# Half-rows of conditioning moved from an RWKV layer into the MLP before it

## The chip, the core and the metric

The kernel runs on one core of one Trainium2 chip. The metric is the device time of one execution in microseconds; the median of several executions is compared. The engines are named as in the profile: PE is the matrix engine (PEld are its weight loads), DVE the vector engine, ACT the scalar engine, POOL the GpSimd engine, SP the engine whose queue issues nearly all DMA transfers here.

## What is computed

Two layers of an encoder on 256 tokens of width 2048, in float32. Each layer has a mixing part and an MLP of width 8192, and each of these four parts is conditioned: a vector c gives a shift, a scale and a gate per channel.

```
def adaln(x, c, norm_g, ada_w, ada_b):
    m = jax.nn.silu(c) @ ada_w + ada_b
    shift, scale, gate = jnp.split(m[:, None, :], 3, axis=-1)
    return rmsnorm(x, norm_g) * (1.0 + scale) + shift, gate

def sqrelu_mlp(h, w1, w2):
    return jnp.square(jax.nn.relu(h @ w1)) @ w2
...
        h, gate = adaln(x, c, tm_norm_g[i], tm_ada_w[i], tm_ada_b[i])
        y = rwkv7_block(h, ...)
        x = x + gate * y
        h, gate = adaln(x, c, ffn_norm_g[layer], ffn_ada_w[layer], ffn_ada_b[layer])
        x = x + gate * sqrelu_mlp(h, ffn_w1[layer], ffn_w2[layer])
```

The order of the parts is: mixing of layer 0 (a long convolution and a linear attention; "mix"), first MLP ("f0"), mixing of layer 1 (RWKV-7; "tm"), second MLP ("f1"), final norm. The conditioning matrix of each part is 2048 x 6144, so its product with silu(c) reads 50 MB for one vector; it depends on c alone and can be done at any time before the part needs it.

## The kernel before

**The conditioning in half-rows.** The matrix of each part is stored transposed and cut into tiles of 128 x 1024, 512 KB each, called half-rows here. A third of a part (0 shift, 1 scale, 2 gate) has 32 of them. `ada_load` issues the transfer of the next one on SP's queue into the pool `wp` (6 buffers); `ada_half` multiplies it on DVE with silu(c), which lies broadcast in SBUF, and sums along the row (line 362, one SCALAR_TENSOR_TENSOR). After each four columns of 128 the sums get their bias in a few small operations (lines 367 to 370). `bg` does one half-row: it keeps up to AP = 5 transfers ahead and then multiplies the oldest.

**When half-rows are done.** Each weight load (`load`, line 494) adds half the rate of the part to a counter in `tick`, and each whole unit calls `bg`. The rate of the first MLP is RF0 = 1.2, that of the second RF1 = 0.8. The first MLP's counter starts at DV = -12. In the RWKV layer the rate is 0, and the loop over pairs of heads calls `bg` instead: from pair 3 to pair 14, up to 10 or 5 times a pair (`bg_gen`, table BG). Which half-row comes next is set in `ada_load`: first the gate of the part that is running, once its shift and scale are done; then, over all parts in order, shift and scale. The gate of a later part is therefore never loaded before that part runs.

**The MLP.** `ffn` works in two halves. Each half has 8 blocks of w1 (`feat_block`, 8 weight tiles of 128 x 1024 each) and 4 blocks of w2 (`tok_block`, 16 tiles each): 256 weight tiles in an MLP. Every tile is split into a high part (a cast on ACT, line 465) and the rest (a subtraction on DVE, line 466), into three pairs of buffers, and each product is three matmuls (lines 510 to 512). Weight tiles go to 7 buffers of their own and, each seventh, to `wp`. The names are f_w (a tile, a weight's or a half-row's), f_wh and f_wl (its parts), f_h (normed input), f_hid (hidden).

**The RWKV layer.** After the norm, projections and a stretch of preparation comes a loop over 16 pairs of heads. In it `weave` mixes five streams: the chain of one pair (states Q, masks M, S), the preparation of the next, the tail of the one before, the linear blocks (`rw_v`, `rw_o`, three tiles loaded ahead into `wp`) and the half-rows. tm_M is a masked score of a pair, written by DVE (line 1506) and read by PE (line 1561). The gate is spread over the tokens after the last pair (`spread_gate`) and used in the residual.

**The order.** The program is written as above; a scheduler then sets the order of each engine's instructions. In a run each engine, and SP's queue, goes through its list in order: an instruction that waits holds up all behind it.

Of the kernel before, what the change touches and what calls it, by code (L numbers as in the profile page):

```python
# [25 lines left out]
SUBS = ("mix", "f0", "tm", "f1")  # L26
FX, FN, NU, XD = 2, 3, 0, 4
PT = ("0111111", "0111")
RHY, RGL, RWO, RF0, RF1 = 2.4, 2, 0.6, 1.2, 0.8
HA, HB, HN, HT = 1000, 1000, 0, 0  # L30
LG, MK, XS, TB, DU, RP, IB, L1, MP, AP = 2, 7, 4, 0, -8.0, 1, 3, 0, 3, 5
W1, W2 = 1, 1
BG, IV, CH, MT, B0, B1, M0, M1, LD = (10, 10, 10, 10, 10, 10, 10, 10, 10, 5, 5, 5, 5, 5, 5, 5, 5, 5), 12, 7, (5, 5, 5, 5, 5, 5, 5, 5, 5, 5, 5, 2, 3, 2, 3, 2, 3, 2), 3, 14, 6, 6, 6
PK, PF = 8, 3
RH, ZZ = (0, 2.4, 2, 2), 0
NF, F1, TF = 2, 2, 0
PR, PQ = 'mppp', 'mppp'
# [176 lines left out]
class Build:  # L214
# [21 lines left out]
    def run(self):  # L236
        nc, ctx, A = self.nc, self.ctx, self.A
        self.const = self.pool(ctx, "const")
        self.wp = self.pool(ctx, "wp", bufs=6)
        self.due, self.rate, self.turn, self.hold, self.starting = 0.0, 0.0, 0, None, False  # L240
        self.cut, self.casts, self.wq = None, [], None
        self.small = self.pool(ctx, "small", bufs=2)
        self.tmp = self.pool(ctx, "tmp", bufs=4)
        self.gstack = ctx.enter_context(ExitStack())
        self.open_gate()
        self.wstack = ctx.enter_context(ExitStack())
        self.open_work()
        self.mm = self.pool(ctx, "mm", bufs=4, space=PSUM)
        self.q = {"sp": nc.sync, "act": nc.scalar, "pool": nc.gpsimd}[QM]
        self.pstack = ctx.enter_context(ExitStack())  # L250
        self.open_ps(4)
        self.xstack = ctx.enter_context(ExitStack())
        self.ada_left = {(s, i): 2 * KT for s in self.stages if s in SUBS for i in range(3)}
        self.ada_next, self.ada_sum, self.ada_out, self.ada_done = [], {}, {}, {}
        self.label = self.stages[0]
        if self.stages[0] != "mix":
            self.start()
            self.load_x()
        for s in SUBS:
            if s in self.stages:  # L260
                self.label = s
                self.rate = RF0 if s == "f0" else RF1
                if s[0] == "f":
                    self.ffn(s)
                elif s == "mix":
                    self.mix()
                else:
                    self.rwkv()
        self.final()
# [43 lines left out]
    def ada_load(self):  # L313

        left, s = self.ada_left, self.label
        todo = [(s, 2)] if not left.get((s, 0)) and not left.get((s, 1)) else []
        if s == "mix" and left.get((s, 0)):
            todo = [(s, 0 if left[s, 0] % 2 or left[s, 0] == left[s, 1] else 1)]
        if self.starting:
            todo = [("mix", i) for i in range(2)] if not todo or todo[0][1] == 2 else todo  # L320
        else:
            todo += [(q, i) for q in SUBS for i in range(2)]
        for u in todo:
            if left.get(u):
                w = self.t(self.wp, [P, D // 2], "w")
                i, j = divmod(2 * KT - left[u], 2)
                self.nc.sync.dma_start(w, self.A["ada_" + u[0]][u[1] * KT + i][:, j])
                left[u] -= 1
                return *u, i, w, j
# [83 lines left out]
    def norm_t(self, s, split=True):  # L413
        h, step = self.norm_steps(s, split)
        for k2 in range(KT // 2):
            step(k2)
        return (lambda k: [a[:, k % 8, :] for a in h[k // 8]]) if split else h
# [44 lines left out]


    def split(self, a, hi, lo, eng=None):
        c = self.nc.scalar.copy(hi, a)  # L465
        d = (eng or self.nc.vector).tensor_tensor(lo, a, hi, ALU.subtract)  # L466
        if eng is None:
            self.cut = d.ins
            self.casts = [c.ins]

    def behind(self):

# [15 lines left out]
    def load(self, name, n, i, pools):  # L488

        self.turn += 1  # L490
        w = self.t(pools[self.turn % len(pools)], [P, 2, NB], "w")
        src = self.A[name][n, i // 2][:, i % 2 * 2 : i % 2 * 2 + 2]
        if self.wq is None:
            self.dma = self.nc.sync.dma_start(w, src).ins
        else:
            with self.tc.issue_after(self.casts[-1]):
                self.wq.dma_start(w, src)
        self.tick(self.rate / 2)
        return w

# [551 lines left out]
    def rwkv_out(self, yd, ns, k0, k1, pts, pool):  # L1052
# [18 lines left out]
        def ahead(u):  # L1071
            i, n = units[u]
            if i not in x:
                x.clear()
                x[i] = [self.t(self.xt, [P, 2, T], t, dt=F32R) for t in ("xh", "xl")]
                y = self.t(self.xt, [P, 2, T], "xu", bufs=2)
                nc.sync.dma_start(y, yd[:, 2 * i : 2 * i + 2, :])
                self.split(y, *x[i], nc.gpsimd)
            if u + 1 < len(units):
                load(u + 1)  # L1080
            v = [self.t(self.ws, [P, 2, NB], t, dt=F32R) for t in ("wh", "wl")]
            self.split_weights(w[u], v)
            return x[i], v

        def ready(u):
            return u == len(units) or self.tails >= min(2 * units[u][0] + 2, 14)

        load(0)
        while not ready(0):
            yield 1  # L1090
# [13 lines left out]
    def rwkv(self):  # L1104
# [12 lines left out]
        with ExitStack() as st:  # L1117
# [37 lines left out]
            with ExitStack() as st2:  # L1155
                self.hp = self.pool(st2, "hp", bufs=4, reuse_waits="tile")
                h, norm = self.norm_steps("tm", False)
                xx = [self.t(self.hp, [P, 8, T], "h") for _ in range(2)]
                for k2 in range(8):
                    norm(k2)  # L1160
                    a, o = (z[k2 // 4][:, 2 * k2 % 8 : 2 * k2 % 8 + 2] for z in (h, xx))
                    (nc.vector if k2 < XD else nc.gpsimd).tensor_tensor(o[:, :, 1 : T - 1], a[:, :, : T - 2], a[:, :, 2:], ALU.add)
                    nc.gpsimd.tensor_copy(o[:, :, 0], a[:, :, 1])
                    nc.gpsimd.tensor_copy(o[:, :, T - 1], a[:, :, T - 2])
                    nc.vector.scalar_tensor_tensor(o, o, 0.5, a, ALU.mult, ALU.subtract)
                nc.scalar.dma_start(xs, self.x)
                self.xstack.close()
                self.rate, self.wq = 0.0, None
                mixes = self.spill_mixes(h, xx)
                for _ in range(8):  # L1170
                    next(mixes)
                self.weave((self.lora(h, xx), 16), (mixes, 16), (self.take(mains, 35), 35))
# [23 lines left out]
            with ExitStack() as st1:  # L1196
# [69 lines left out]
                w = None  # L1266
                for n in range(4):
# [3 lines left out]
                    w = self.load("rw_o", n, KT // 2 - 1, [self.wp])  # L1271
# [3 lines left out]
                        for m in range(2):  # L1275
                            self.prod(pts[n][m], [a[:, k, m * P : (m + 1) * P] for a in y], [a[:, k, :] for a in v], False, k == 1)
                    self.residual("tm", n, pts[n])
        self.wq = None
        self.open_gate()
        self.open_work()  # L1280

# [444 lines left out]
```

## Time and profile before

| | before |
|---|---|
| median of 3 runs | 3051.21 us (3048.9 to 3052.1) |
| profiled execution | 3047.34 us, span 3045.3 us |
| PE busy, weight loads | 2871.4 us (94%), 2488.7 us (82%) |
| DVE busy | 2122.1 us (70%) |
| ACT busy | 1301.6 us (43%) |
| POOL busy | 522.2 us (17%) |
| moved by DMA | 752.30 MB, mean 247 GB/s |

The span is from the first instruction to the last; the profiled execution's own time is 2.0 us more. Busy shares are averages over stages of different kind. Line numbers are those of the kernel before.

### The profile page before, as it was taken

Reading aid. Unit: us, or ns where it says so; the run is one execution under the profiler, and the core shown is the slowest. Engines: PE = TensorE matmul, PEld = TensorE weight load, DVE = VectorE, ACT = ScalarE, POOL = GpSimd, SP = SyncE. Lnnn points to the kernel's source line nnn. Section 1 sums busy time; section 2 is a strip of 40 time slices with the busy share of each in tenths; the row PEclk is TensorE's granted clock in tenths of the full one; section 3 lists DMA queues with packets and bytes.
Section 4 is the critical chain, followed back from the end, with each engine's and each line's share of the span. In section 5 each row is a group of like instructions: output and inputs, shape, how many; then the busy total and the mean of one; then the engine's idle time right before and its main releaser. Section 6 shows DMA issues by size and latency. Waiting matters only on the chain. (4 is left out here: it accounts for less than half of the span.)

```text
span 3045.3 us, 52042 instructions
## 1 busy us (share of the span) xinstructions
PE 2871.4 (94%) x20308; PEld 2488.7 (82%) x20308; DVE 2122.1 (70%) x3126; ACT 1301.6 (43%) x1947; POOL 522.2 (17%) x574
## 2 busy tenths in 40 slices
PE   6999989999999999997999878999998999999998
PEld 2678776789988999886888777777778998899986
DVE  7899866657777788787768875775646776455454
ACT  3233334444443444443466542334445443344443
POOL 1211200011100011004354541322322110001000
PEclk9999999999999999998999987999999999999999
DMA  9978777747898988984987788997545777555552
GB/s 328 326 271 284 243 262 263 247 154 244 287 308 306 304 290 290 313 297 158 323 264 249 266 258 226 301 300 208 149 149 194 245 252 272 193 186 183 202 193 93
DMA packets 279970, 752.30 MB, mean 247 GB/s; under 512 B 73081, under 2 KB 99577, under 8 KB 278572
## 3 DMA queue, kind: packets, MB, share of 16 engines
q1 hardware_dynamic: 279148, 745.38, 73.1%
q8 instruction: 159, 2.61, 0.3%
q10 hardware_dynamic: 576, 3.60, 0.3%
q14 instruction: 87, 0.71, 0.1%
HBM read 706.08 MB, written 42.80 MB: 246 GB/s over the span
## 5 line engine op out<-in xcount | busy, mean ns | idle before, releaser
L466 DVE TENSOR_TENSOR f_wl<-f_w,f_wh 128x1024 fp32r<-128x1024 f32 x512 | 630.8, 1233 | 444.3 <-ACT f_wh L465 433.4
L465 ACT CAST f_wh<-f_w 128x1024 fp32r<-128x1024 f32 x512 | 538.0, 1052 | 748.4 <-PE f_mm L512 315.8
L511 PE MATMUL f_mm<-f_h,f_wh 128*128 128x256 f32 x2048 | 579.5, 283 | 0.0
L510 PE MATMUL f_mm<-f_h,f_wh 128*128 128x256 f32 x2048 | 579.5, 283 | 0.0
L512 PE MATMUL f_mm<-f_h,f_wl 128*128 128x256 f32 x2048 | 579.1, 283 | 0.0
L511 PE MATMUL f_mm<-f_wl,f_hid 128*128 128x512 f32 x1024 | 398.6, 389 | 1.1 <-DVE f_wl L466 1.1
L512 PE MATMUL f_mm<-f_wh,f_hid 128*128 128x512 f32 x1024 | 398.5, 389 | 0.0
L511 PEld LDWEIGHTS f_mm<-f_h,f_wh 128*128 128x128 f32 x2048 | 393.2, 192 | 0.1
L510 PEld LDWEIGHTS f_mm<-f_h,f_wh 128*128 128x128 f32 x2048 | 393.0, 192 | 0.1
L512 PEld LDWEIGHTS f_mm<-f_h,f_wl 128*128 128x128 f32 x2048 | 392.9, 192 | 0.0
L510 PE MATMUL f_mm<-f_wh,f_hid 128*128 128x512 f32 x1024 | 357.9, 389 | 0.0
L362 DVE SCALAR_TENSOR_TENSOR mix_w<-mix_w,mix_s 128x1024 f32<-128x1024 f32 x175 | 219.8, 1265 | 77.0 <-DMA mix_w<-in_ada_f 52.5
L466 POOL TENSOR_TENSOR f_hid<-f_u,f_hid 128x512 fp32r<-128x512 f32 x64 | 98.0, 1531 | 990.6 <-ACT f_hid L465 988.2
L362 DVE SCALAR_TENSOR_TENSOR f_w<-f_w,mix_s 128x1024 f32<-128x1024 f32 x174 | 233.6, 1345 | 2.6 <-DMA f_w<-in_ada_f 2.6
L511 PEld LDWEIGHTS f_mm<-f_wl,f_hid 128*128 128x128 f32 x1024 | 192.2, 188 | 41.3 <-DVE f_wl L466 1.7
L512 PEld LDWEIGHTS f_mm<-f_wh,f_hid 128*128 128x128 f32 x1024 | 192.3, 188 | 39.8
L510 PEld LDWEIGHTS f_mm<-f_wh,f_hid 128*128 128x128 f32 x1024 | 192.2, 188 | 39.7
L466 DVE TENSOR_TENSOR tm_wl<-tm_w,tm_wh 128x1024 fp32r<-128x1024 f32 x128 | 164.4, 1287 | 85.8 <-ACT tm_wh L465 81.6
L465 ACT CAST mix_wh<-mix_w 128x1024 fp32r<-128x1024 f32 x114 | 119.4, 1050 | 201.2 <-PE mix_mm L512 86.3
L510 PE MATMUL tm_mm<-tm_x,tm_wh 128*128 128x256 f32 x512 | 161.2, 316 | 12.3 <-DMA tm_x<-mix 10.8
L465 ACT CAST tm_wh<-tm_w 128x1024 fp32r<-128x1024 f32 x128 | 133.4, 1046 | 86.7 <-PE tm_mm L511 60.3
L466 DVE TENSOR_TENSOR mix_wl<-mix_w,mix_wh 128x1024 fp32r<-128x1024 f32 x114 | 142.4, 1254 | 38.8 <-ACT mix_wh L465 38.7
(456 smaller groups left out, 5494.6 us busy)
## 6 DMA issues: line engine op xcount, KB each, us to landing
f_w<-in_w SPq DMA_DIRECT2D x512, 512.0 KB, 5.1
f_w<-in_ada_f SPq DMA_DIRECT2D x125, 512.0 KB, 5.6
mix_w<-in_ada_mix SPq DMA_DIRECT2D x96, 512.0 KB, 6.2
mix_w<-in_w_in SPq DMA_DIRECT2D x80, 512.0 KB, 5.0
mix_w<-in_ada_f SPq DMA_DIRECT2D x64, 512.0 KB, 5.2
tm_x<-mix SPq DMA_DIRECT2D x64, 512.0 KB, 5.8
f_w<-in_ada_tm SPq DMA_DIRECT2D x49, 512.0 KB, 5.8
mix_w<-in_w_out SPq DMA_DIRECT2D x32, 512.0 KB, 4.6
```

The source lines that it names most:

```text
L362: V.scalar_tensor_tensor(w, w, 1.0, self.s[:, j * (D // 2) : (j + 1) * (D // 2)], ALU.mult, ALU.mult, accum_out=a[:, j, i : i + 1])
L465: c = self.nc.scalar.copy(hi, a)
L466: d = (eng or self.nc.vector).tensor_tensor(lo, a, hi, ALU.subtract)
L510: mm(out, lhsT=l[0], rhs=r[0], start=start, stop=False)
L511: mm(out, lhsT=l[0], rhs=r[1], start=False, stop=False)
L512: mm(out, lhsT=l[1], rhs=r[0], start=False, stop=stop)
```

## The change

Three numbers and one line. RF0 becomes 1.5, so that in the first MLP two weight loads call for 1.5 half-rows where they called for 1.2. In `ada_load` the list for the part s takes the third 2 (the gate) of a later part q as well where (s, q) stands in the new table EARLY, which holds the first MLP and the RWKV layer. A way of issuing weight loads from another queue, which was never switched on (`wq` was None throughout), is taken out.

```
-RHY, RGL, RWO, RF0, RF1 = 2.4, 2, 0.6, 1.2, 0.8
+RHY, RGL, RWO, RF0, RF1 = 2.4, 2, 0.6, 1.5, 0.8
...
-PK, PF = 8, 3
+PK, PF, EARLY = 8, 3, (("f0", "tm"),)
...
         if self.starting:
             todo = [("mix", i) for i in range(2)] if not todo or todo[0][1] == 2 else todo
         else:
-            todo += [(q, i) for q in SUBS for i in range(2)]
+            todo += [(q, i) for q in SUBS for i in range(3 if (s, q) in EARLY else 2)]
...
-        src = self.A[name][n, i // 2][:, i % 2 * 2 : i % 2 * 2 + 2]
-        if self.wq is None:
-            self.dma = self.nc.sync.dma_start(w, src).ins
-        else:
-            with self.tc.issue_after(self.casts[-1]):
-                self.wq.dma_start(w, src)
+        self.dma = self.nc.sync.dma_start(w, self.A[name][n, i // 2][:, i % 2 * 2 : i % 2 * 2 + 2]).ins
         self.tick(self.rate / 2)
```

By the program, the half-rows loaded in the first MLP were 32 of its own gate, 49 of tm's shift and scale and 61 of f1's, 142 in all; they are now 32, 81 (49 and the 32 of tm's gate) and 64, 177 in all. In the RWKV layer there were 35 (32 of the gate, 3 of f1's scale); there are none now, and the calls of `bg` from the loop find nothing to do. The other parts keep theirs.

The order of DVE in the last quarter of the first MLP, in a block of w2, before (L466 splits a weight tile, L362 multiplies a half-row, L367 and L368 are the small sums):

```order
L466 TENSOR_TENSOR f_wl_10884<-f_w_10876,f_wh_10883 128x1024
L367 TENSOR_TENSOR f_ss_1588_9409<-f_as_9408 128x4
L368 TENSOR_TENSOR f_ss_1588_9409<-f_ss_1588_9409,mix_pv_93 128x4
L466 TENSOR_TENSOR f_wl_10902<-f_w_10899,f_wh_10901 128x1024
L362 SCALAR_TENSOR_TENSOR f_w_10779,f_as_10921<-f_w_10779,mix_s_96 128x1024
L466 TENSOR_TENSOR f_wl_10925<-f_w_10917,f_wh_10924 128x1024
L362 SCALAR_TENSOR_TENSOR f_w_10818,f_as_10921<-f_w_10818,mix_s_96 128x1024
L466 TENSOR_TENSOR f_wl_10946<-f_w_10940,f_wh_10945 128x1024
L466 TENSOR_TENSOR f_wl_10964<-f_w_10961,f_wh_10963 128x1024
```

and the same place now (lines have moved by up to seven, and buffers have other numbers):

```order
L466 TENSOR_TENSOR f_wl_10985<-f_w_10979,f_wh_10984 128x1024
L362 SCALAR_TENSOR_TENSOR f_w_10900,f_as_9886<-f_w_10900,mix_s_96 128x1024
L367 TENSOR_TENSOR f_ss_1662_9887<-f_as_9886 128x4
L466 TENSOR_TENSOR f_wl_11008<-f_w_11000,f_wh_11007 128x1024
L362 SCALAR_TENSOR_TENSOR f_w_10921,f_as_11027<-f_w_10921,mix_s_96 128x1024
L368 TENSOR_TENSOR f_ss_1662_9887<-f_ss_1662_9887,mix_pv_93 128x4
L466 TENSOR_TENSOR f_wl_11031<-f_w_11023,f_wh_11030 128x1024
L466 TENSOR_TENSOR f_wl_11049<-f_w_11046,f_wh_11048 128x1024
L362 SCALAR_TENSOR_TENSOR f_w_10942,f_as_11027<-f_w_10942,mix_s_96 128x1024
```

Where about three of five splits were followed by a multiplication, three of four are now.

The order of DVE in the RWKV loop, at the first tiles of a block of rw_v, before (tm_wl is the rest of a weight tile, tm_M a masked score that PE waits for, tm_gn belongs to a pair's tail):

```order
L466 TENSOR_TENSOR tm_wl_18681<-tm_w_18670,tm_wh_18680 128x1024
L1506 TENSOR_TENSOR tm_M_18868<-tm_ps_18869,tm_rc_11838 128x4x2x64
L1506 TENSOR_TENSOR tm_M_18868<-tm_ps_18870,tm_rc_11838 128x4x2x64
L466 TENSOR_TENSOR tm_wl_18777<-tm_w_18672,tm_wh_18776 128x1024
L362 SCALAR_TENSOR_TENSOR tm_w_18704,tm_as_18151<-tm_w_18704,mix_s_96 128x1024
L1506 TENSOR_TENSOR tm_M_18792<-tm_mm_18794,tm_rc_11838 128x4x2x64
L1640 TENSOR_SCALAR tm_gn_18887<-tm_mm_18851 128x256
L362 SCALAR_TENSOR_TENSOR tm_w_18748,tm_as_18151<-tm_w_18748,mix_s_96 128x1024
```

and now, at the first tiles of the same block:

```order
L466 TENSOR_TENSOR tm_wl_18742<-tm_w_18731,tm_wh_18741 128x1024
L1499 TENSOR_TENSOR tm_M_18507<-tm_mm_18509,tm_rc_11956 128x4x2x64
L1565 TENSOR_SCALAR tm_Q_18119<-tm_ps_18523 64x128
L1499 TENSOR_TENSOR tm_M_18507<-tm_ps_18508,tm_rc_11956 128x4x2x64
L1633 TENSOR_SCALAR tm_gn_18593<-tm_mm_18560 128x256
```

The multiplications are gone from between the scores and the splits, and the block's first split stands at another score of the chain.

The order of SP's queue around the first load of that block, before (L327 is a half-row, L494 a weight tile; the rest are small loads and stores of the pairs):

```order
L327 DMA tm_w_18646<-in_ada_tm 128x1024
L1601 DMA tm_bon_19372<-ab_11791 128x256
L1009 DMA tm_x_18906<-mix_11784 128x1024
L1452 DMA tm_bk_18715<-ab_11793 128x2x512
L1460 DMA tm_N_18721<-nd_11803 128x2x256
L494 DMA tm_w_18670<-in_rw_v 128x1024
```

and now:

```order
L1435 DMA rx_11927<-tm_E_17990 16x4x1024
L1435 DMA rt_11931<-tm_E_17990 16x4x1024
L491 DMA tm_w_18731<-in_rw_v 128x1024
L1462 DMA tm_T_17723<-rt_11929 32x4x32 x4
L1003 DMA tm_x_17962<-mix_11902 128x1024
L306 DMA tm_x_18768<-x_spill 128x4096
L491 DMA tm_w_18733<-in_rw_v 128x1024
L1451 DMA tm_pc_18094<-ab_11909 64x2x4 x2
```

With the half-rows gone from `wp`, the block's loads stand some 24 entries earlier in the queue, ahead of loads of the pairs that they used to follow.

## Rows read from the trace of the kernel before

**Rows 1.** The page: span, and busy time of each engine (share of span).

```profile
span 3045.3 us, 52042 instructions
...
PE 2871.4 (94%) x20308; PEld 2488.7 (82%) x20308; DVE 2122.1 (70%) x3126; ACT 1301.6 (43%) x1947; POOL 522.2 (17%) x574
```

**Rows 2.** Windows: from:to, length, busy (records) PE PEld DVE ACT POOL; clock, DMA.

```profile
654.00:841.00 187.00, 187.00 (x1564) 187.00 (x1564) 135.46 (x155) 87.72 (x106) 33.34 (x22) 1.00 0.73 245
841.00:1017.00 176.00, 176.00 (x801) 146.64 (x800) 135.81 (x180) 70.55 (x70) 4.87 (x2) 1.00 0.90 310
1017.00:1202.00 185.00, 185.00 (x1530) 184.38 (x1529) 147.67 (x173) 82.36 (x93) 20.59 (x14) 1.00 0.87 293
1202.00:1379.00 177.00, 177.00 (x793) 146.81 (x791) 136.46 (x176) 72.45 (x79) 2.89 (x2) 1.00 0.86 295
...
1896.60:2049.60 153.00, 146.40 (x1839) 121.79 (x1833) 116.48 (x240) 59.62 (x152) 42.53 (x63) 0.97 0.95 296
2050.60:2122.90 72.30, 72.30 (x893) 55.27 (x894) 41.15 (x94) 32.86 (x83) 21.13 (x37) 1.00 0.75 222
2122.90:2203.80 80.90, 79.67 (x1118) 61.95 (x1119) 49.72 (x119) 37.52 (x104) 25.53 (x45) 1.00 0.56 157
```

**Rows 3.** Tile f_mm on PE, first, then second MLP: count, ns min/median/max, first and last start.

```profile
L510 PE MATMUL f_mm<-f_h,f_wh x1024: 278/283/365, 654.8 to 1204.4; 128*128 128x256 f32 x171
...
L512 PE MATMUL f_mm<-f_wh,f_hid x512: 388/389/476, 845.0 to 1378.7; 128*128 128x512 f32 x171
...
L510 PE MATMUL f_mm<-f_h,f_wh x1024: 278/283/364, 2306.8 to 2858.2; 128*128 128x256 f32 x171
...
L512 PE MATMUL f_mm<-f_wh,f_hid x512: 387/389/397, 2497.2 to 3032.5; 128*128 128x512 f32 x171
```

**Rows 4.** Line 362 (multiplication of half-rows): first MLP, second MLP, RWKV loop.

```profile
L362 DVE SCALAR_TENSOR_TENSOR f_w<-f_w,mix_s x142: 1211/1219/2323, 733.5 to 1371.3; 128x1024 f32<-128x1024 f32 x142
...
L362 DVE SCALAR_TENSOR_TENSOR f_w<-f_w,mix_s x32: 1212/1218/2324, 2367.7 to 2546.2; 128x1024 f32<-128x1024 f32 x32
...
L362 DVE SCALAR_TENSOR_TENSOR tm_w<-tm_w,mix_s x35: 1203/1218/2136, 1902.7 to 2048.4; 128x1024 f32<-128x1024 f32 x35
```

**Rows 5.** Waits of PE, 1896.6 to 2049.6: us in total, times, longest.

```profile
PE tm_mm L1561 <- DVE tm_M L1506: 3.5, 1, 3.5
PE tm_ps L1561 <- ACT tm_Q L1590: 1.5, 2, 1.0
PE tm_mm L510 <- ACT tm_wh L465: 1.3, 1, 1.3
PE tm_ps L1571 <- ACT tm_R L1563: 0.4, 1, 0.4
```

**Rows 6.** Timeline of DVE: start, us; in brackets idle before it and what ended it.

```profile
1981.94 1.23 DVE L466 TENSOR_TENSOR tm_wl<-tm_w,tm_wh 128x1024 fp32r<-128x1024 f32 x1
1987.83 1.23 DVE L362 SCALAR_TENSOR_TENSOR tm_w<-tm_w,mix_s 128x1024 f32<-128x1024 f32 x1 [4.66 <-DMA tm_w<-in_ada_tm]
...
1988.98 0.69 DVE L1506 TENSOR_TENSOR tm_M<-tm_mm,tm_rc 128x512 f32<-128x512 f32 x1
```

**Rows 7.** Windows of 2 us around that wait, columns as in rows 2.

```profile
1988.00:1990.00 2.00, 0.28 (x5) 0.28 (x6) 2.00 (x4) 0.00 (x0) 0.59 (x1) 0.68 0.50 138
1990.00:1992.00 2.00, 2.00 (x16) 1.66 (x16) 0.58 (x1) 1.15 (x4) 0.62 (x2) 0.50 0.80 223
...
1996.00:1998.00 2.00, 2.00 (x40) 2.00 (x39) 1.08 (x1) 0.00 (x0) 0.00 (x0) 0.50 1.05 391
1998.00:2000.00 2.00, 2.00 (x23) 1.50 (x19) 1.11 (x5) 1.07 (x3) 0.47 (x3) 0.76 1.03 408
```

**Rows 8.** The page, DMA issues: count, size, us to landing.

```profile
f_w<-in_w SPq DMA_DIRECT2D x512, 512.0 KB, 5.1
```

**Rows 9.** Windows at the program's start, columns as in rows 2.

```profile
20.00:40.00 20.00, 13.30 (x17) 5.06 (x18) 14.41 (x35) 11.74 (x24) 0.00 (x0) 1.00 1.03 386
```

**Rows 10.** Waits of PE, 2049.6 to 2202.8.

```profile
PE tm_ps L1582 <- DVE tm_M L1506: 0.6, 1, 0.6
PE tm_ps L1535 <- DVE tm_Y L1528: 0.5, 1, 0.5
```

More of the change, by code (lines that the diff above doesn't have):

```diff
@@ L240, in run @@
         self.due, self.rate, self.turn, self.hold, self.starting = 0.0, 0.0, 0, None, False
-        self.cut, self.casts, self.wq = None, [], None
+        self.cut = None
         self.small = self.pool(ctx, "small", bufs=2)
@@ L464, in split @@
     def split(self, a, hi, lo, eng=None):
-        c = self.nc.scalar.copy(hi, a)
+        self.nc.scalar.copy(hi, a)
         d = (eng or self.nc.vector).tensor_tensor(lo, a, hi, ALU.subtract)
@@ L468, in split @@
             self.cut = d.ins
-            self.casts = [c.ins]
     def behind(self):
@@ L1167, in rwkv @@
                 self.xstack.close()
-                self.rate, self.wq = 0.0, None
+                self.rate = 0.0
                 mixes = self.spill_mixes(h, xx)
@@ L1277, in rwkv @@
                     self.residual("tm", n, pts[n])
-        self.wq = None
         self.open_gate()
```

## The prediction

> **What bounds the kernel now.** I read the page first: one profiled execution of 3047.34 us, 3045.3 us of it the span, TensorE (PE) busy for 94%, VectorE (DVE) for 70% [rows 1]. The chain that ended last explains only a quarter of the span, so I went on by stretches. That execution lies 3.9 us below the median of the runs shown, 3051.21 us; I make the sum on the profile and take it off the median.
>
> The stretches [rows 2] are the first MLP's four quarters (its two halves, w1 then w2 in each) and three stretches of the RWKV layer's loop over pairs. The reader is to see that PE is busy for the whole of every MLP quarter, 187.00 us of 187.00 and so on, while DVE has 37 to 52 us free in each. PE sets the time there. The direct proof is the second MLP, the same work on other weights: from the start of the first matmul to the start of the last, the first MLP takes 654.8 to 1378.7, 723.9 us, the second 2306.8 to 3032.5, 725.7 us [rows 3]. DVE multiplied 142 half-rows of the first MLP's own loading during the one and 32 during the other [rows 4]. So 110 half-rows more cost nothing that can be seen.
>
> The gate's half-rows stand in the RWKV loop: 35 multiplications from 1902.7 to 2048.4 us [rows 4] (32 of the gate, 3 of the last MLP's conditioning). I take the stretch from 1896.6 to 2049.6: PE busy 146.40 of 153.00 us, DMA share 0.95, mean clock 0.97 [rows 2]. PE's waits in it add up to 6.7 us, the longest 3.5 us for a tm_M of DVE [rows 5]. The timeline says why DVE was late [rows 6]: it had nothing running from 1983.2 and then sat 4.66 us before a half-row's multiplication, until the transfer of that half-row landed; the tm_M stood behind it in DVE's queue and started at 1988.98. While PE was idle the granted clock fell: 0.68 from 1988 to 1990, 0.50 in the next four windows of 2 us, 0.76 from 1998 to 2000 [rows 7]. That is the level of 1.2 GHz; PE had stood idle before it fell, and had worked on without such a wait when 2.4 GHz came back.
>
> **The change part by part.** *The first MLP gains 35 half-rows.* By the order of DVE its multiplications grow from 146 to 181 (four of either were loaded earlier), by quarter from 26, 39, 39, 42 to 36, 48, 48, 49.
> On DVE: 35 of 1.22 us [rows 4] are 43 us. The four quarters hold 555 us of DVE work in 725 [rows 2]; 598 us are 82%. In a w2 quarter nine more make 136 us into 147 of 176. There is at most one tick of conditioning per weight load and the load's period there is 176/64 = 2.75 us, against one split and one multiplication of about 1.2 us each, so the lag does not grow from load to load. Cost taken: nothing, hidden under PE; without that cover it would be the 43 us.
> On the DMA queue: 256 weight loads and 177 half-rows of 0.524 MB each [rows 8] are 227 MB, over 723.9 us 314 GB/s, against 288 with 142. The tightest stretch is a w2 quarter: 64 loads and 48 half-rows, 58.7 MB in 176 us, 334 GB/s. The quarter of 841 to 1017 us moved 310 at a share of 0.90, which is 344 at a full share [rows 2], and at the program's start the same kind of transfers ran at 386 for 20 us [rows 9]. So it fits, by 3% at the nearer row. Bounds: nothing below, and above, if the MLP held only the 310 of its best quarter, 227/310 = 732 us, 8 us more. I take nothing, because the second MLP, with 110 half-rows less to move, is no shorter.
>
> *The RWKV stretch loses 35 multiplications (43 us of DVE), 35 transfers of 512 KB and their issues on SP, and eight sets of small sums.* PE's work there is the same, so only what PE loses can be won. The idle time first: 6.7 us of waits [rows 5]. The stretch of the same length behind it, which has pairs and weight loads but no half-row, has waits of 1.1 us [rows 10]. Difference 5.6 us. Three of the four waits have the half-rows as their cause by what stands in the queues: the tm_M directly; the 1.3 us for tm_wh because the first weights of a value block are issued behind half-row loads in SP's queue (in the new order they stand ahead of the pair's other loads); the tm_Q because its DVE sources take turns with the multiplications. Then the clock: the windows of 2 us lost 0.32 + 4 x 0.50 + 0.24 = 2.56 shares, 5.1 us, of which 0.6 us fell where PE was idle for 1.7 us anyway [rows 7]; 4.5 us.
> Bounds: above, a stretch without half-rows packs its matmul records more densely, 1118 in 80.90 us against 1839 in 153.00 [rows 2]; at that density the stretch would be 133 us, 20 us less, but the mix of matmuls differs (fewer of the long ones later), so this is an end and not the value. Below, nothing is won if another wait takes the place of the 3.5 us and lets the clock fall as well.
>
> *Nothing else moves.* The order is the same on all engines from the first MLP's end to the stretch, and again from its end to the second MLP, apart from a few neighbours exchanged; the gate's columns are complete long before the residual needs them. The second MLP has its 32 half-rows as before.
>
> Sum: 0 - 5.6 - 4.5 = -10.1 us; 3051.2 - 10.1 = 3041.1, so **3041 us**.
>
> By the Trainium skill (Perfetto Trace Analysis, Identifying the Most-Contended Engine) the busy share of matmuls is a poor measure of TensorE's headroom and that of weight loads a good one. By it the stretch, at 121.79 of 153.00 us, stands well below the first MLP at 665 of 725, and filling it to that share would take 20 us off: 3031 us. The trace speaks against it: in the two stretches behind, with no half-rows, the weight loads' share is not higher but lower, 55.27 of 72.30 and 61.95 of 80.90 us [rows 2].
>
> **The rivals.** *More comes back (0.10).* If DVE's turns delayed many of the chain's small steps by less than the profile counts as a wait, the stretch shrinks by 13 to 20 us: 3031 to 3038. For it: 35 multiplications of 1.22 us stand among the chain's short steps, and the density above. Against it: PE is already busy for 146.40 of 153.00 us [rows 2], and the later pairs have fewer of the long matmuls. The rule of the Trainium skill's page named above would end at the far end of this case.
>
> *A new wait takes its place (0.24).* The pieces are woven anew: in the new DVE order a tm_wl, which waits for a cast and so for a load of rw_v, stands directly ahead of a tm_M, as the multiplication did. If that load lands 4 us late once, PE idles 3 to 4 us and the clock falls again: 8 us of the 10.1 are gone, 3047 to 3051, no change. Against it: the loads of rw_v now stand earlier in SP's queue and 18 MB of traffic are gone from a stretch at a DMA share of 0.95.
>
> *The first MLP pays (0.08, the other side).* Its place is the DMA queue. If it can hold only what the last three quarters moved on the mean, 299 GB/s [rows 2], 227 MB take 759 us: 35 us more, less 10.1, 3076 us. It decides for slower when the MLP is over 740 us, that is, below 307 GB/s. Against it: 310 in one quarter, 386 at the start, and shares below 1.
>
> That the half-rows stay in the RWKV layer is excluded by the order, which has none there.
>
> **How the numbers follow.** My forecast has 0.58: 3039 to 3045 us. A measurement of this kernel tells a change from none at about 0.2%, 6.1 us: faster is below 3045.1, slower above 3057.3. Faster takes 0.56 of my forecast and the 0.10; same its last 0.02 and the 0.24; slower 0.08. The range of 3034 to 3052 leaves out the far half of the first rival and all of the third, some 0.13; it holds both bounds of the first MLP (0 and 8 us) and those of the stretch but for the last 3 us of 20.
>
> **What would show it.** Right: the first MLP's first to last matmul again 724 us within 2, PE busy throughout, DMA near 314 GB/s; no multiplication of half-rows between 1379 and 2300 us; PE's waits from pair 2 to pair 6 at some 1 us and no clock below 1.00 there; the distance from the first MLP's last matmul to the second's first 10 us shorter than 928.1 us. Wrong: an MLP longer than 727 us with waits of PE for f_wl or f_wh; a clock dip in the loop; a tm_M behind a late tm_wl.

## The result, and the profile after

| | before | after |
|---|---|---|
| median | 3051.65 us (4 runs, 3048.9 to 3057.89) | 3033.48 us (4 runs, 3030.18 to 3037.25) |
| ratio | | 0.9947, 95% interval 0.9935 to 0.9959 |
| profiled execution, its span | 3047.34 us, 3045.3 us | 3034.37 us, 3032.4 us |

The change makes the kernel faster, by 16 us as the ratio has it (12 to 20 by its interval). The forecast was 3041 us, in a range of its own from 3039 to 3045; the ratio, put on the 3051.2 us that the forecast started from, gives 3035. The page of the changed kernel begins (compare [rows 1]):

```profile
span 3032.4 us, 52074 instructions
...
PE 2861.2 (94%) x20308; PEld 2481.7 (82%) x20308; DVE 2114.9 (70%) x3126; ACT 1301.1 (43%) x1947; POOL 514.6 (17%) x574
```

The shares are those of before; as before, they hide the stage that matters. The windows of the first MLP's four quarters, and below them the RWKV loop from pair 0 to pair 6 (columns as in [rows 2]). Pair 0 to pair 6 is meant here and below from the first matmul that makes pair 0's output (line 1616 before, 1609 after) to the first that makes pair 6's:

```profile
658.20:839.00 180.80, 180.80 (x1514) 180.80 (x1513) 141.30 (x176) 85.44 (x104) 31.27 (x22) 1.00 0.79 270
839.00:1020.00 181.00, 181.00 (x843) 151.53 (x842) 147.36 (x200) 71.87 (x71) 2.89 (x2) 1.00 0.93 336
1020.00:1201.00 181.00, 181.00 (x1495) 180.30 (x1494) 154.07 (x191) 80.96 (x91) 20.53 (x14) 1.00 0.92 319
1201.00:1382.10 181.10, 181.10 (x829) 151.21 (x829) 146.56 (x196) 73.29 (x80) 2.95 (x2) 1.00 0.91 320
1890.90:2035.40 144.50, 144.50 (x1939) 122.70 (x1936) 80.92 (x184) 65.17 (x161) 37.78 (x67) 1.00 0.76 227
```

The reader is to see two things. In the MLP, DVE has more to do and DMA moves 270 to 336 GB/s, and PE is still busy for the whole of every quarter. In the loop DVE has fallen to 81 us, the DMA share to 0.76, and PE has no idle time and no clock under 1.00. The kernel before, in the same piece of work:

```profile
1887.50:2048.10 160.60, 154.00 (x1942) 128.71 (x1940) 121.53 (x258) 64.28 (x160) 42.39 (x67) 0.97 0.94 291
```

160.60 against 144.50: 16.1 us, for nearly the same matmuls (1942 and 1939 records). The tile f_mm on PE, of the first MLP and then of the second (as in [rows 3], first and last start):

```profile
L504 PE MATMUL f_mm<-f_h,f_wh x1024: 278/283/363, 658.2 to 1207.9; 128*128 128x256 f32 x171
...
L506 PE MATMUL f_mm<-f_wh,f_hid x512: 388/389/402, 850.2 to 1382.1; 128*128 128x512 f32 x171
...
L504 PE MATMUL f_mm<-f_h,f_wh x1024: 277/283/364, 2294.1 to 2845.4; 128*128 128x256 f32 x171
...
L506 PE MATMUL f_mm<-f_wh,f_hid x512: 387/389/398, 2484.8 to 3019.6; 128*128 128x512 f32 x171
```

The first MLP takes 1382.1 - 658.2 = 723.9 us, to the tenth what it took before, and the second 725.5. Between them lie 912.0 us, 16.1 less than the 928.1 of before: all of it is the loop from pair 0 to pair 6. (The first MLP starts 3.4 us later; that arises ahead of anything that was changed, and the same kernel taken again, e_again below, starts it at 655.3.) Line 362 on DVE has 177 multiplications in the first MLP, and no row with a tm_w (compare [rows 4]):

```profile
L362 DVE SCALAR_TENSOR_TENSOR f_w<-f_w,mix_s x177: 1210/1218/2332, 719.0 to 1373.9; 128x1024 f32<-128x1024 f32 x177
...
L362 DVE SCALAR_TENSOR_TENSOR f_w<-f_w,mix_s x32: 1211/1218/2324, 2355.3 to 2533.3; 128x1024 f32<-128x1024 f32 x32
```

### The profile page after: what moved, and what is told of

It reads as the page before. It is cut to its first block, busy times and chain, and to the rows that moved or that the text cites. A ratio compares the mean times of both kernels' runs of the same rounds, so it can differ in the third digit from the quotient of the medians.

```text
span 3032.4 us, 52074 instructions
## 1 busy us (share of the span) xinstructions
PE 2861.2 (94%) x20308; PEld 2481.7 (82%) x20308; DVE 2114.9 (70%) x3126; ACT 1301.1 (43%) x1947; POOL 514.6 (17%) x574
## 5 line engine op out<-in xcount | busy, mean ns | idle before, releaser
L466 DVE TENSOR_TENSOR f_wl<-f_w,f_wh 128x1024 fp32r<-128x1024 f32 x512 | 633.7, 1239 | 412.7 <-ACT f_wh L465 408.3
L362 DVE SCALAR_TENSOR_TENSOR f_w<-f_w,mix_s 128x1024 f32<-128x1024 f32 x209 | 275.1, 1317 | 1.7 <-DMA f_w<-in_ada_f 1.7
L362 DVE SCALAR_TENSOR_TENSOR mix_w<-mix_w,mix_s 128x1024 f32<-128x1024 f32 x175 | 220.5, 1269 | 76.6 <-DMA mix_w<-in_ada_f 49.2
L466 POOL TENSOR_TENSOR f_hid<-f_u,f_hid 128x512 fp32r<-128x512 f32 x64 | 94.2, 1472 | 995.4 <-ACT f_hid L465 990.5
L466 DVE TENSOR_TENSOR tm_wl<-tm_w,tm_wh 128x1024 fp32r<-128x1024 f32 x128 | 164.9, 1290 | 85.3 <-ACT tm_wh L465 82.1
L504 PE MATMUL tm_mm<-tm_x,tm_wh 128*128 128x256 f32 x512 | 160.6, 314 | 11.8 <-DMA tm_x<-mix 11.3
L466 DVE TENSOR_TENSOR mix_wl<-mix_w,mix_wh 128x1024 fp32r<-128x1024 f32 x114 | 142.4, 1254 | 38.8 <-ACT mix_wh L465 38.6
```

The lines of the kernel that those rows point to most:

```text
L362: V.scalar_tensor_tensor(w, w, 1.0, self.s[:, j * (D // 2) : (j + 1) * (D // 2)], ALU.mult, ALU.mult, accum_out=a[:, j, i : i + 1])
L504: mm(out, lhsT=l[0], rhs=r[0], start=start, stop=False)
```

## The experiments

The gain of 16 us was 6 more than the sum. Three explanations stood at the start: the waits for a half-row's transfer (theory 1, the prediction's own), DVE's turns (theory 2), the traffic (theory 3); two came later. All kernels but e_thin are the changed kernel with something put back or set anew. Ratios are against runs of the kernel before on the same chip; "between" is from the first MLP's last f_mm to the second's first, in the profiled execution.

| kernel | what stands in the loop | median, us | ratio to before (95%) | between | pairs 0 to 6 |
|---|---|---|---|---|---|
| before | 35 half-rows | 3048.4 to 3051.7 | | 928.1 | 160.6 |
| after | nothing | 3033.48 | 0.9947 (0.9935 to 0.9959) | 912.0 | 144.5 |
| e_again | nothing | 3030.89 | 0.9941 (0.9927 to 0.9955) | 911.5 | 144.5 |
| e_slot | 35 empty turns | 3032.42 | 0.9940 (0.9928 to 0.9953) | 911.8 | 144.5 |
| e_one | 4 multiplications | 3035.22 | 0.9952 (0.9938 to 0.9967) | 914.3 | 144.6 |
| e_mul | 35 multiplications | 3048.32 | 1.0002 (0.9992 to 1.0013) | 927.5 | 157.5 |
| e_half | the same, at half as many turns a pair | 3046.14 | 0.9987 (0.9978 to 0.9997) | 925.1 | 157.6 |
| e_quart | the same, in 140 pieces | 3050.12 | 1.0001 (0.9992 to 1.0011) | 931.9 | 163.3 |
| e_load | 35 transfers | 3051.36 | 1.0007 (0.9996 to 1.0018) | 931.7 | 161.4 |
| e_both | both, on separate data | 3052.59 | 1.0018 (1.0007 to 1.0029) | 929.0 | 165.3 |
| e_rate | the gate's 32 half-rows | 3057.80 | 1.0030 (1.0017 to 1.0043) | 931.4 | 168.6 |
| e_early | 35 half-rows, f1's | 3048.73 | 1.0003 (0.9990 to 1.0015) | 927.2 | 160.8 |
| e_thin | 35 half-rows over 12 pairs | 3061.04 | 1.0043 (1.0025 to 1.0062) | 938.5 | 158.5 |
| e_rf2 | nothing; first MLP crowded | 3060.79 | 1.0033 (1.0017 to 1.0048) | 913.2 | 144.3 |

### Multiplications alone (e_mul)

In `bg_gen`, with `again` at 35 when the loop begins and `fake` a small tile for the sums:

```
-            if self.bg():
+            if self.again:
+                self.again -= 1
+                i, j = divmod(self.again, 2)
+                c = slice(j * (D // 2), (j + 1) * (D // 2))
+                o = self.t(self.wp, [P, D // 2], "w")
+                self.nc.vector.scalar_tensor_tensor(o, self.s[:, c], 1.0, self.s[:, c], ALU.mult, ALU.mult, accum_out=self.fake[:, i : i + 1])
                 yield 1
```

> The changed kernel with 35 multiplications of the half-row's size put back into the RWKV loop on DVE, at the turns that the conditioning had there, but on data that lie in SBUF since the start: no transfer, no wait for one. Their products are not used by the output. Numbers: the whole time (before 3051.65 us, after 3033.48), and the distance from the first MLP's last matmul to the second's first (before 928.1, after 912.0). Theory 1 (the cost was DVE standing before a half-row until its transfer landed, with the short steps behind it, and the fall of the clock that followed): 912 to 914, time 3033 to 3036, no granted clock under 1.00 in the loop. Theory 2 (43 us of DVE's turns in the loop held up short steps a little each, under what the trace counts as a wait; some 5 us of the gain that the predicted sum did not have): 916 to 919, time 3037 to 3041. Theory 3 (the transfers held up other loads): as theory 1 here.

Nearly the whole gain is gone, with no transfer in the loop: 927.5 us between the MLPs. Theory 1 falls as the whole cause; theory 2 has the right cause and less than half the size. The window of pairs 0 to 6, and the windows of 2 us from 1944 on:

```profile
1890.60:2048.10 157.50, 154.38 (x1935) 128.62 (x1931) 120.91 (x255) 65.25 (x161) 46.04 (x67) 0.98 0.71 208
```

```profile
1946.00:1948.00 2.00, 0.82 (x5) 0.71 (x6) 1.94 (x4) 0.00 (x0) 1.47 (x3) 0.72 0.90 256
1948.00:1950.00 2.00, 2.00 (x13) 1.71 (x14) 1.08 (x5) 1.20 (x4) 0.56 (x1) 0.50 0.85 231
1950.00:1952.00 2.00, 2.00 (x13) 1.66 (x14) 0.96 (x4) 0.87 (x1) 0.17 (x1) 0.50 0.92 327
1952.00:1954.00 2.00, 2.00 (x24) 1.35 (x23) 1.97 (x2) 0.27 (x1) 0.00 (x0) 0.57 1.09 304
```

The timeline ahead of the fall, DVE and PE (start, us; in brackets the idle time before it and what ended it):

```profile
1943.26 1.22 DVE L352 SCALAR_TENSOR_TENSOR tm_w<-mix_s 128x1024 f32<-128x1024 f32 x1
...
1944.40 1.22 DVE L352 SCALAR_TENSOR_TENSOR tm_w<-mix_s 128x1024 f32<-128x1024 f32 x1
...
1945.55 0.69 DVE L1505 TENSOR_TENSOR tm_M<-tm_ps,tm_rc 128x512 f32<-128x512 f32 x1
1946.15 0.42 DVE L1642 SCALAR_TENSOR_TENSOR tm_gn<-tm_gn,tm_gn 128x256 f32<-128x256 f32 x1
1946.60 0.52 DVE L1590 COPY tm_Q<-tm_S 64x128 f32<-64x128 f32 x1
...
1947.17 0.69 PE L1560 MATMUL tm_ps<-tm_Q,tm_M 128*64 128x64 f32 x4 [1.32 <-DVE tm_Q L1590]
```

DVE waited for nothing here: two multiplications in a row and two further steps stood ahead of the copy of tm_Q, and PE idled 1.32 us for it. The clock then fell to its lower level, and pair 1 took 33.6 us instead of 23.4. The multiplications also stood nearer together than they had: by their starts 5, 14, 6, 6 and 4 in pairs 0 to 4, where the kernel before has 2, 6, 7, 6, 6 and 7 in pairs 0 to 5 and one behind. Their products go to buffers of `wp`, as the half-rows did, so that they could also hold up the weights of rw_v; but no wait of PE here is for a weight's part, and of its weight loads' waits the longest for one is 0.3 us.

The 13.0 us over the changed kernel's 144.5 come in three parts: 3.1 of idle PE (157.50 - 154.38); the clock, 0.28 + 0.50 + 0.50 + 0.43 = 1.71 shares of 2 us, 3.4 us, of which some 0.3 fell where PE was idle anyway; and 6.8 us in which PE counts as busy at full clock.

### Transfers alone (e_load)

```
+                w = self.t(self.wp, [P, D // 2], "w")
+                self.nc.sync.dma_start(w, self.A["ada_tm"][2 * KT + i % KT][:, j])
```

in place of the multiplication above.

> The changed kernel with 35 transfers of half-rows (512 KB each) put back into SP's queue in the RWKV loop, at the turns of before, and nothing that reads them: added traffic, not used by the output. Theory 1 (waits for a transfer's landing): distance between the MLPs 912 to 914 us, time 3033 to 3036. Theory 2 (DVE's turns): the same, 912 to 914. Theory 3 (the transfers fill the DMA engines, 0.95 of them before, and hold up the loads and spills that the loop itself waits for): 916 to 919, time 3037 to 3041, DMA share in the loop back at about 0.95 and PE waiting for DMA-fed tiles there.

931.7 us: all the gain is gone again, by another way. Theory 3 is right in that transfers alone cost the gain, and they cost more than it expected. The waits of PE in pairs 0 to 6 and the windows:

```profile
PE tm_mm L508 <- ACT tm_wh L469: 3.9, 1, 3.9
PE tm_ps L1569 <- ACT tm_R L1561: 3.7, 1, 3.7
```

```profile
1887.50:2048.90 161.40, 152.64 (x1931) 129.76 (x1927) 79.94 (x184) 63.33 (x159) 35.51 (x67) 0.94 0.91 280
```

ACT's timeline says why both were late:

```profile
1971.11 0.62 ACT L469 CAST tm_xh<-tm_xu 128x512 fp32r<-128x512 f32 x1 [5.23 <-DMA tm_xu<-y_spill]
1971.75 0.27 ACT L1561 COPY tm_R<-tm_ps 128x128 f32<-128x128 f32 x1
...
1983.04 1.04 ACT L469 CAST tm_wh<-tm_w 128x1024 fp32r<-128x1024 f32 x1 [2.19 <-DMA tm_w<-in_rw_v]
```

The shape is that of [rows 6], on another engine: ACT sat 5.23 us before a cast whose input had not landed, the short copy of tm_R stood behind it, and PE waited for that. Later a weight of rw_v was late. Between 1971 and 1993 all eleven windows of 2 us show a clock under 1.00. Idle PE is 8.8 us here, and the three pairs before the first fall take what they take in the changed kernel (27.4, 23.4 and 23.2 us against 27.5, 23.4 and 23.2), though 15 of the 35 transfers were issued in them: transfers alone leave nothing in PE's busy time. SP's own queue stood still as well until half-rows had landed that nothing reads; the largest of these waits (us in total, times, longest):

```profile
SPq L1007 <- DMA tm_w<-in_ada_tm: 4.5, 3, 2.1
SPq L1550 <- DMA tm_w<-in_ada_tm: 3.8, 3, 1.9
```

In all they are 22.1 us, with 30.9 us more for other transfers; in the same pairs of the changed kernel SP waits 5.3 us for transfers. Whether late data come from the full DMA engines or from this queue was not told apart.

### Both, on separate data (e_both)

The two edits together; the multiplication reads resident data, not what was loaded. Its product, though, goes to a buffer of `wp`, the pool into which the half-rows are loaded.

> The changed kernel with both put back into the RWKV loop, 35 transfers and 35 multiplications, but the multiplications read data that lie in SBUF, so that none waits for a transfer (the products and the transfers are not used by the output). Theory 1: 912 to 915 us between the MLPs, time 3033 to 3037, no clock under 1.00 in the loop; what is then left to the 3051.65 of before is the wait alone. Theories 2 and 3: 916 to 919, time 3037 to 3041. If the sum of work and traffic is what counts, whatever waits for what: 925 to 928, time 3047 to 3052.

929.0 us and 3052.59: 1 us above the third line of the expectation. The kernel is not the test that it was meant to be, for its multiplications did wait for transfers: DVE's largest wait for one, and around 1958 us DVE and then PE (start, us; in brackets the idle time before it and what ended it):

```profile
DVE tm_w L354 <- DMA tm_w<-in_ada_tm: 8.5, 6, 2.5
```

```profile
1957.88 1.23 DVE L354 SCALAR_TENSOR_TENSOR tm_w<-mix_s 128x1024 f32<-128x1024 f32 x1 [2.47 <-DMA tm_w<-in_ada_tm]
...
1959.75 0.23 DVE L1592 COPY tm_Q<-tm_S 64x128 f32<-64x128 f32 x1
...
1960.03 0.45 PE L1562 MATMUL tm_ps<-tm_Q,tm_M 128*64 128x64 f32 x4 [1.63 <-DVE tm_Q L1592]
```

This is the case of [rows 6] once more (there 13.1 us of such waits in pairs 0 to 6, in eight). So e_both says nothing against theory 1; e_mul, with no transfer for a multiplication to wait for, does. What e_both shows is the sum: the loop takes 165.3 us, more than with either alone, and the losses overlap rather than add.

### One part of the change at a time (e_rate and e_early)

e_rate has EARLY empty:

```
-PK, PF, EARLY = 8, 3, (("f0", "tm"),)
+PK, PF, EARLY = 8, 3, ()
```

> One part of the change alone: 1.5 half-rows per two weight loads in the first MLP, but the gate's 32 half-rows stay in the RWKV loop, each multiplication waiting for its own transfer as before; the first MLP does the 3 half-rows of the last MLP's conditioning besides its own. All theories expect nearly the time of before, 3045 to 3052 us, 924 to 928 us between the MLPs; theory 1 ties it to places: a wait of DVE of 2 us or more before a half-row, a wait of PE behind it, then the clock at half. Where no wait of PE in the loop is longer than 2 us, theory 1 expects 916 to 922 and 3037 to 3043; theory 2 expects the loss of 5 us even then and has no price for the rest.

e_early has the old rate:

```
-RHY, RGL, RWO, RF0, RF1 = 2.4, 2, 0.6, 1.5, 0.8
+RHY, RGL, RWO, RF0, RF1 = 2.4, 2, 0.6, 1.2, 0.8
```

> The other part of the change alone: the gate is allowed in the first MLP, but at 1.2 half-rows per two weight loads as before, so that its 32 half-rows take the place of 35 others there, and 35 multiplications with their transfers are still in the RWKV loop, for the last MLP. All theories: as before, 3045 to 3055 us, 924 to 932 us between the MLPs, pairs 0 to 6 at 157 to 168 us with a fall of the clock. 3035 or less would say that it matters whose half-rows they are.

Neither part alone gains anything. e_early came as expected. e_rate is slower than before, by 0.3%, more than any theory had: the clock fell at 1969 us behind a wait of 2.0 us for a tm_Q and stayed under 1.00 for 14 windows of 2 us. DVE's last wait for a half-row ahead of that was 1.3 us, not the 2 us or more that theory 1 had asked for. Both fit a loop that is disturbed by half-rows, whichever they are, the gate's (32 in e_rate) or f1's (35 in e_early): the change gains because it takes them all out.

### The same kernel again, and the turns without work (e_again, e_slot)

e_slot has in `bg_gen`, with `again` at 35 as above,

```
-            if self.bg():
+            if self.again:
+                self.again -= 1
                 yield 1
```

> The changed kernel once more, unchanged, on the chip of the next three: 912 us between the MLPs, time 3031 to 3036 by every theory; its executions should spread less than those of before (3039.6 to 3056.6 in 31 runs) if what spreads them are falls of the clock in the RWKV loop.

> The changed kernel with only the 35 turns put back that the conditioning had in the weave of the RWKV loop, empty: no multiplication, no transfer; the output is unchanged. It asks whether the order of the other work, which those turns shift, is what cost the time. Theory 4 (with half-row work in the loop some short step comes 1 to 4 us late, whichever it is, TensorE stands, and its clock falls to half for 6 us or more; besides, the multiplications delay many steps by fractions of a microsecond): 912 to 914 between the MLPs, time 3031 to 3037, no clock under 1.00 in pairs 1 to 6. Theory 5 (the order of the instructions does it): 922 or more, 3043 or more.

Both take 144.5 us for pairs 0 to 6 and 911.5 and 911.8 between the MLPs. Empty turns cost nothing, so theory 5 falls as it was put; but they hardly move the order of PE either (under "Still open"), so other orders are not tested by this. The executions spread over 3028.2 to 3038.1 and 3029.3 to 3034.4 us (5 each), those of before over 3044.4 to 3054.2 (15) on the same chip: e_again's five spread as widely as the fifteen of before, so falls of the clock in the loop are not shown to be what spreads them.

### Smaller pieces, few pieces, lower density (e_quart, e_one, e_half, e_thin)

e_quart cuts each multiplication into four of 256 columns, at 40 turns a pair instead of 10 (`again` begins at 140):

```
-                c = slice(j * (D // 2), (j + 1) * (D // 2))
+                c = slice(self.again % 4 * (D // 8), (self.again % 4 + 1) * (D // 8))
...
-                        ... (self.bg_gen(bg), bg) if B0 <= p <= B1 ...
+                        ... (self.bg_gen(4 * bg), 4 * bg) if B0 <= p <= B1 ...
```

e_one does four whole multiplications at the turn p = 5 of the loop and none at another; the turns themselves stay (`again` begins at 4):

```
-            if self.again:
+            while self.again and p == 5:
```

> The 35 multiplications on resident data as before (their products are not used by the output), but each cut into four of a quarter of the columns, 140 in all, at 140 turns of the loop. By theory 4 with the length of one piece as what delays: the delays shrink with the piece, no wait of TensorE of 1 us, no clock under 1.00, 912 to 917 between the MLPs, time 3032 to 3039. By theory 4 with the sum of DVE's time as what delays: as with the whole pieces, 922 to 930, time 3043 to 3050.

> Four multiplications on resident data (4.9 us of DVE) in one pair of the loop alone, close together; products not used by the output. Theory 4: where they stand before a short step that TensorE waits for, that pair takes 30 to 36 us instead of 23 to 25, with a wait of 1 to 4 us and then the clock at half, and the other pairs are as in the changed kernel: 918 to 925 between the MLPs, time 3038 to 3046. If only the sum of the 43 us matters: 913 to 914, 3033 to 3037.

e_quart: 163.3 us; smaller pieces do not help. PE's longest waits there are 1.5 and 1.4 us, and the clock fell behind them twice in the loop. e_one: 144.6 us, as if nothing had been added; DVE's slack took 4.9 us without a trace, and theory 4's 30 us for that pair was wrong. (The 2.3 us more between the MLPs stand behind the last pair: PE waits 9.8 us there for f_dg, 9.7 in e_slot and 7.9 in the changed kernel.) Its four multiplications start within 6.4 us of one pair. So density was the next theory: e_half gives the multiplications 5 turns a pair (`bg // 2` for `bg` in the line above), e_thin is the kernel before with

```
-BG, ... = (10, 10, 10, 10, 10, 10, 10, 10, 10, 5, 5, 5, 5, 5, 5, 5, 5, 5), ...
+BG, ... = (3,) * 18, ...
```

> The changed kernel with the 35 multiplications on resident data (products not used by the output) at 5 a pair, half the density of the first such kernel, which took 157.4 us for pairs 0 to 6. Density theory: 144.5 to 149 for pairs 0 to 6, time 3031 to 3040. Sum theory: some 13 us more than the changed kernel over pairs 0 to 9, time 3044 to 3050.

> The kernel before with one thing changed: the same 35 half-rows, transfers, waits and all, stand in the RWKV loop at 3 for each of 12 pairs instead of 10 a pair. The loop without any of them takes 144.5 us for pairs 0 to 6, in three kernels to the 0.1 us; with 35 of them in four or five pairs 157.4 to 168.6. If the density is what costs (theory 4: short steps come late only where several half-rows stand between them, and four in one pair cost nothing): pairs 0 to 6 144.5 to 148, no wait of 1 us, no clock under 1.00, time 3030 to 3038, as good as the changed kernel. If each half-row costs its part wherever it stands (16 us over 35): 925 to 930 between the MLPs, time 3045 to 3052.

It fell in both. e_half's window and PE's waits in it:

```profile
1887.00:2044.60 157.60, 155.76 (x1953) 130.73 (x1951) 117.31 (x249) 66.25 (x161) 45.45 (x68) 1.00 0.71 205
```

```profile
PE tm_ps L1570 <- ACT tm_R L1562: 0.8, 2, 0.5
PE tm_ps L1560 <- ACT tm_Q L1589: 0.6, 1, 0.6
PE tm_ps L1570 <- ACT tm_bkt L1513: 0.4, 1, 0.4
```

This row is the most telling of all. No clock under 1.00, 1.84 us of idle PE, "busy" for 99%, and 13.1 us longer than the changed kernel: 11.3 us of it stand inside PE's busy time. About 1.4 us of these are more work and no delay: twelve more matmuls of the linear blocks fall into the window (360 against 348), at 0.12 us each, as in [rows 2] (1564 in 187.00 us). Nor did halving the turns halve the density everywhere: by their starts DVE has 5, 4, 3, 4, 10 and 5 multiplications in pairs 0 to 5 and four behind. Pair 1, with four, took 28.0 us instead of 23.4.

e_thin loses in pairs 0 to 6 (158.5 us) and again behind them, where the changed kernel takes 183.0 us and it takes

```profile
2039.50:2233.50 194.00, 184.88 (x2323) 140.98 (x2322) 118.16 (x272) 84.22 (x220) 55.44 (x91) 0.98 0.60 178
```

Its DVE sat 16 times, 26.4 us in all, before a half-row, and three of its 35 multiplications came only behind the last pair; so of the two it is e_half that speaks to density alone.

### The first MLP crowded (e_rf2)

RF0 = 2.0 in place of 1.5.

> The changed kernel at 2.0 half-rows per two weight loads, so that the first MLP's loads are crowded into its first two thirds or so at a demand of some 380 GB/s. If the transfers have no room there (386 GB/s was the most that the program's start reached, [rows 9]): waits of TensorE for f_wl or f_wh in the first MLP, which takes 728 to 745 us, time 3038 to 3052. If they have: 724 us there, and time 3031 to 3036.

The first MLP takes 1407.4 - 657.3 = 750.1 us, more than the 728 to 745 expected, and the time is 3060.79. Waits of PE in it, and its windows from 842 to 1110:

```profile
PE f_mm L506 <- DVE f_wl L466: 5.9, 12, 1.3
PE f_mm L504 <- ACT f_wh L465: 5.6, 10, 1.0
PE f_mm L505 <- DVE f_wl L466: 3.8, 8, 0.5
```

```profile
842.00:930.00 88.00, 84.76 (x411) 69.89 (x410) 76.52 (x109) 33.60 (x35) 3.70 (x2) 1.00 0.97 365
930.00:1020.00 90.00, 87.77 (x379) 70.29 (x379) 79.49 (x114) 32.16 (x32) 0.00 (x0) 1.00 0.98 361
1020.00:1110.00 90.00, 87.50 (x651) 83.03 (x650) 75.92 (x108) 34.41 (x37) 5.34 (x4) 1.00 0.97 358
```

So the cover under PE holds, but not for much more: at 336 GB/s in its tightest quarter the changed kernel pays nothing, at 358 to 365 with a share of 0.97 the weights come late. Again PE's waits (15.3 us) are less than what the MLP lost (26.2).

## Why the prediction was right, and where it was too small

**The first MLP at nothing: right.** 723.9 us against 723.9, PE busy throughout, 311 GB/s over its quarters (mean of the four rows by length) where 314 was worked out, and 336 in the tightest where 334 was. The rival by which it pays was excluded by that; e_rf2 shows that it would have come true at a higher rate.

**No new wait: right.** The rival with a tm_wl ahead of a tm_M did not come. PE has no wait in the loop's window at all. The order is there, but the weights are in time: the DMA share is 0.76.

**The stretch at -10.1 us: mis-sized; it was -16.1.** Of the 160.60 us of before, 6.60 are idle PE (154.00 busy); all of that went, where the sum left 1.1 of it, so this term was -6.6 instead of -5.6. The clock's term of 4.5 us [rows 7] went as a whole. That leaves 16.1 - 6.6 - 4.5 = 5.0 us that no wait and no clock of [rows 5, 7] shows. The step that failed is the argument against the first rival, "PE is already busy for 146.40 of 153.00 us": it took busy time for work that cannot shrink. e_half shows some 10 us of such delay at full clock and e_mul 6.8, while e_load has next to none; so it comes with DVE's multiplications, as that rival had it. The rival "more comes back", 13 to 20 us, at a chance of 0.10, was the case that came. By the ratio the time is 3035 us (the median of the four runs is 3033.48): below the 3039 to 3045 that had 0.58, and at the lower end of the whole range of 3034 to 3052. That the range reached so far down it owes to that rival and not to the sum, so for the size it was luck.

**The cause was told too narrowly.** The 3.5 us for tm_M, with DVE sitting before a transfer [rows 6], were taken as the mechanism. They were one instance. With the transfers gone (e_mul) a tm_Q came late behind DVE's turns; with the multiplications gone (e_load) a tm_R behind a late transfer on ACT; in each PE idled 1.3 to 3.9 us once or twice and the clock fell behind it. To take away the one wait of the profile would have gained little: in e_mul no multiplication has a transfer to wait for, and it is as slow as before.

By the Trainium skill (Perfetto Trace Analysis, Identifying the Most-Contended Engine) matmul busy time does not say how near TensorE is to its best; the share of peak FLOPs that is reached and weight loads' busy time do. The runs agree with the first half: 99% busy in e_half, 13.1 us too long. As for weight loads, their share of pairs 0 to 6 is 0.80 before, 0.83 in e_half and 0.85 after. It moves the right way, but it is 0.85 with nothing left to wait for and not the 0.92 of the first MLP, so filling to that share was too much to hope for, as the prediction said.

**Still open.** What the 5 to 10 us inside the busy time are. The traces show where they stand. A record of PE lasts 0.2 to 0.5 us and overlaps the next, so a matmul that starts a tenth of a microsecond late leaves PE "busy". Counted by the starts of PE's records in pairs 0 to 6, 895 of 1,936 follow the one before within 0.05 us in the changed kernel and 804 of 1,950 in e_half; steps of 0.05 to 0.25 us take 118.5 us in the one and 129.3 us in the other. So the loss is many short steps and not a few waits.

What makes these steps longer was not told apart. The scheduler set PE's order anew wherever multiplications stood in the loop: by the order of their starts, of some 4,350 matmuls from pair 0's first output to pair 15's last about 1,300 stand elsewhere in e_mul, e_half and before than in the changed kernel, and fewer than 40 in e_slot and e_one. It may be that order, or DVE's turns themselves; a kernel with the one order and the other's work was not tried. e_load, with some 720 moved, lost nothing that way, so a new order does not cost by itself. That four multiplications in one pair are free and 35 cost 13 us, in e_mul's spread and in e_half's, is shown; where between them it begins is not.

## What to carry to other kernels

In this kernel filler work belonged under the stage that one engine fills with long, regular instructions, and had to leave the stage of short dependent steps almost wholly: with one side of it changed (its transfers, its multiplications, its turns a pair, its piece size, its source) 4 us at most were gained, with all of it gone 16, and with four multiplications left in the loop nearly as much. When a profile shows one late step, ask whether it is the cause or the first of many that are nearly late; a kernel without the suspected cause tells, once its trace has shown that the cause is gone (in e_both it was not). And price a stage by the same work without the filler, not by the waits that are listed: here 5 to 10 us stood inside "busy".

## What was not expected of the hardware

A single wait of PE of 1.32 us was followed by the lower clock for over 5 us (e_mul, 1.2 GHz from 1948 to 1952), which cost more than the wait. Waits of like length did not always do that: behind 1.48 us in e_rate (at 2010) and 1.24 us in e_thin (at 1956) the clock stayed at 1.00. In pairs 0 to 6 of e_half, with no single wait above 0.6 us, the clock stayed at 1.00 throughout. And the undisturbed loop repeats to a tenth: 144.5 us in three kernels, 144.3 and 144.6 in two more.
